# A decoder step on one core: the turn of the normed input, and the state products of two heads together

## The chip, the cores and the metric

The kernel runs on one core of one Trainium2 chip. A core has TensorE (PE; its weight loads are shown apart as PEld), VectorE (DVE), ScalarE (ACT), GpSimd (POOL) and SyncE (SP), which here issues most of the loads. The metric is the device time of one execution in microseconds, as the median of several runs. The traces are of one profiled execution.

## The reference, cut to what matters

One step of a decoder layer for 256 prompt tokens and for 64 sample tokens (8 sequences of 8), with shared weights. The input is normed and goes through one wide projection; its columns feed a gated linear attention (DeltaNet, 32 value heads, one 128 x 128 state per head and sequence) and a sparse attention over cached pages; both meet in an output projection.

```python
h = rmsnorm(x, norm_g)
u = einsum('btd,de->bte', h, w_in)          # 2048 -> 23664 columns
...
def step(s, xs):                            # linear attention, per head
    u_c, w_c, attn_c, qg_c, kdec_c, gl_c = xs
    v_new = u_c - einsum('bhcd,bhde->bhce', w_c, s)
    o = einsum('bhcd,bhde->bhce', qg_c, s) + einsum('bhij,bhje->bhie', attn_c, v_new)
    s = s * gl_c[..., None, None] + einsum('bhcd,bhce->bhde', kdec_c, v_new)
    return s, o
...
y = x + (sigmoid(m_a) * (o_a @ w_branch_a) + sigmoid(m_b) * (o_b @ w_branch_b)) @ w_out
```

For the samples the 8 tokens of a sequence are one chunk, so that each head needs one such step per sequence, from a state that is loaded and stored again.

## The kernel before, in words

All 320 tokens are kept turned: 16 blocks of 128 input columns on the partitions, tokens in the free dimension (`hhi`, `hlo`). Each fp32 product of a weight matrix is made of three products of split numbers: the input and the weights are each cut into a high part of the shorter format (`fp32r`) and the rest (`hi` and `lo`). A tile of 128 output columns (`acc`) thus takes 16 blocks x 3 = 48 products on TensorE; 11,952 such products (with those of the three output matrices) are the bulk of its work. SyncE loads the weights in pieces of 1 MB into three buffers (`p_load`), ScalarE makes the high part (`p_hi`, tiles `whi`), VectorE the low one (`p_lo`, `wlo`; the first four on GpSimd), and `p_mm` issues the products.

Everything else runs beside this as streams: generators that yield the engine and the tiles that their next piece needs. `Run.go` picks the next piece at each point: the one that can start first by the times that the class `Clock` keeps from prices of instructions and loads, and among equals the one of lowest rank. The order so found is the order of each engine's instructions. A piece whose data come later on the chip than `Clock` has it makes its engine wait, and all that is queued behind it. `Next` and `Place` stand for the time when a buffer comes free. `clock.cold` doubles the prices of TensorE.

Three places matter here.

The start: three tiles of tokens (128, 128 and 64 rows) are loaded; ScalarE squares and sums (`x_norm`), VectorE makes the reciprocal root (`ss`). `gain` spreads the norm's weights over all partitions with four products of one row (`gps`) into four tiles `gb`. `x_turn` scales a piece of 512 columns by root and weights (even pieces on VectorE, odd ones on ScalarE and GpSimd), TensorE transposes its four blocks into a bank (`tp`), ScalarE takes the high part out (`hhi`), VectorE the low one (`hlo`). A projection product of block k waits until the piece with block k of all three tiles is there.

The set-up of the linear attention (`g_init`): small tables are loaded (`c4`, the packs `gdn` and `gini`), the convolution's weights are transposed into `bank`, and a product with `selp` from the pack `gini` puts the samples' gates into another order.

The linear attention goes through 16 groups of two heads. `conv`, `norms`, `prep` and `inverse` prepare a group, `g2_stream` runs the prompt's four pieces in sequence (`p` for the state's growth, `ps<-st,wq` and `ps<-vnz,at` for the output), and `g3_stream` does the samples: for each head eight products of the loaded states with `wS`, one per sequence, each into 32 rows of one bank (`ps<-sS,wqx`), the difference from `uS` on VectorE (`vS`), the product with `ats` onto the same bank, the eviction (`oS`), and then the states' update through `four`, `vx` and `pu`. `load_state` loads the next state into one of two buffers when a head is done.

Of the kernel before, what the change touches and what calls it, by code (L numbers as in the profile page):

```python
# [10 lines left out]
F32 = mybir.dt.float32  # L11
# [435 lines left out]
def step(ctx: ExitStack, tc: tile.TileContext, I, O):  # L447
# [172 lines left out]
    g1row = x0.tile([1, DM], F32, name="grow", bufs=1)  # L620
    SY.dma_start(g1row, dram(I["norm_g"], [[DM, 1], [1, DM]]))
# [11 lines left out]
    gb = [x0.tile([P, 512], F32, name=f"gb{q}", bufs=1) for q in range(4)]  # L633

    def gain():

        one = x0.tile([1, P], F32, name="one", bufs=1)
        V.memset(one, 1.0)
        for q in range(4):
            yield ("pe", g1row, Next(x0p, "tp"))  # L640
            ps = x0p.tile([P, 4, P], F32, tag="tp", name="gps").rearrange("p a b -> p (a b)")
            T.matmul(ps, one, g1row[:, 512 * q:512 * q + 512], start=True, stop=True)
            yield "dve"
            V.tensor_copy(gb[q], ps)
# [3 lines left out]
    def x_norm(ti):  # L648
        t0, n = TT[ti]
        xt = xts[ti]  # L650
        ss = x0.tile([P, 3], F32, tag="ss", name="ss")
        yield ("act", xt)
# [8 lines left out]
        newton(ss[:n, 1:2], ss[:n, 0:1], ss[:n, 2:3])  # L661
        ev = clock.last
        for q in range(4):
            run.add(x_turn(ti, xt, ss, q), q - 4, ev)
# [3 lines left out]
    def x_turn(ti, xt, ss, q):  # L668

        t0, n = TT[ti]  # L670
        c = slice(512 * q, 512 * q + 512)
        if q % 2:
            yield "act"
            S.activation(xt[:n, c], xt[:n, c], AF.Copy, scale=ss[:n, 1:2])
            yield "pool"
            G_.tensor_tensor(xt[:n, c], xt[:n, c], gb[q][:n], op=OP.mult)
        else:
            yield "dve"
            V.scalar_tensor_tensor(xt[:n, c], xt[:n, c], ss[:n, 1:2], gb[q][:n], op0=OP.mult, op1=OP.mult)
        ev = clock.last  # L680
# [3 lines left out]
        yield ("pe", ev, Next(x0p, "tp"))  # L684
        tp = x0p.tile([P, 4, P], F32, tag="tp", name="tp")
        for k in range(4):
            kk = q * 4 + k
            T.transpose(tp[:, k, :n], xt[:n, kk * P:kk * P + P], ident[:n, :n])
        yield "act"
        hs = hhi[:, 4 * q:4 * q + 4, t0:t0 + n]  # L690
        S.activation(hs, tp[:, :, :n], AF.Copy)
        yield "dve"
        V.tensor_tensor(hlo[:, 4 * q:4 * q + 4, t0:t0 + n], tp[:, :, :n], hs.bitcast(F32), op=OP.subtract)
        turned[i] = True
        hq[q] += 1
        done["h"] += 1
# [1662 lines left out]
```

## Time and profile before

| | |
|---|---|
| median of 3 runs | 2552.23 us (2551.02 to 2553.23) |
| the profiled execution | 2554.88 us, its span 2553.1 us |
| TensorE busy | 2503.2 us (98%), 22,220 instructions |
| VectorE, ScalarE, GpSimd busy | 1642.9, 1400.0, 415.2 us |
| mean granted clock of TensorE | 0.993 |
| 16 DMA engines | 549 MB, 215 GB/s |

An fp32 product is recorded as two passes (two matrix instructions), a transpose or a product of the split format as one. The recorded time of a product overlaps the next one's, so the distance between two starts tells what one costs. The idle time in brackets at the end of a row is that of the engine just before it, with what ended it. All code that passes through the helper of `Clock` has one line (L331), so instructions are told apart by their tiles.

### The profile page before, as it was taken

How to read it: one execution, taken by the hardware profiler on the slowest of the kernel's cores; microseconds unless marked ns; L12 is line 12 of the kernel's file. 1: busy time of each engine (PE TensorE's matmuls, PEld its weight loads, DVE VectorE, ACT ScalarE, POOL GpSimd, SP SyncE). 2: the span in 40 equal slices, each digit the busy share in tenths (PEclk: the TensorE clock that was granted, in tenths of full speed). 3: DMA queues.
4: the chain of work that ended last, by engine and by line, in shares of the span. 5: the costliest groups of instructions: out<-in, count | busy, mean ns of one | idle time of the engine just before them, and what ended most of it. 6: DMA issues, size and time to landing. Idle time of an engine off the chain costs nothing.

```text
span 2553.1 us, 59455 instructions
## 1 busy us (share of the span) xinstructions
PE 2503.2 (98%) x22220; PEld 2326.4 (91%) x22220; DVE 1642.9 (64%) x4090; ACT 1400.0 (55%) x3290; POOL 415.2 (16%) x991
## 2 busy tenths in 40 slices
PE   7999999999999999999999999999999989999999
PEld 5998789888889999999999999998999979999999
DVE  5554446655665555545887888788897875555544
ACT  5553444444444434435788767777787755544443
POOL 2000001000000000001234334243333232000000
PEclk9999999999999999999999999999999989999999
DMA  6757776888876999966455645565456556766564
GB/s 198 240 164 252 239 253 221 292 304 297 299 257 231 328 314 317 329 208 200 137 170 171 197 134 181 162 188 163 144 161 200 176 166 199 238 185 185 182 195 127
DMA packets 553796, 549.12 MB, mean 215 GB/s; under 512 B 32995, under 2 KB 457108, under 8 KB 553124
## 3 DMA queue, kind: packets, MB, share of 16 engines
q1 hardware_dynamic: 538660, 496.30, 60.8%
q0 software_dynamic: 14848, 49.04, 5.3%
q8 instruction: 175, 2.87, 0.4%
q14 instruction: 113, 0.92, 0.1%
HBM read 472.93 MB, written 72.29 MB: 214 GB/s over the span
## 4 chain that ended last, share of the span: by engine, by line
PE 73%; issue 17%; DVE 4%; POOL 3%; DMA 1%; ACT 1%; SPq 1%; POOLq 0%; DVEq 0%; ACTq 0%
PE acc L331 55%; PE ps L331 6%; PE nt L331 3%; PE op L331 1%; PE pp L331 1%; POOL vx L331 1%; PE ns L331 1%; PE bank L331 1%; PE p L331 1%; PE pu L331 1%; POOL d_mz L299 1%; DVE wlo L331 1%; PE tp L331 1%; PE ms L331 1%; SPq L299 1%
## 5 line engine op out<-in xcount | busy, mean ns | idle before, releaser
L331 PE MATMUL acc<-hhi,whi 128*128 128x320 f32 (+1 forms) x3472 | 1149.3, 331 | 0.5 <-ACT hhi L331 0.5
L331 PE MATMUL acc<-hhi,wlo 128*128 128x320 f32 (+1 forms) x3472 | 1077.7, 310 | 0.0
L331 PE MATMUL acc<-hlo,whi 128*128 128x320 f32 (+1 forms) x3472 | 1076.9, 310 | 0.1
L331 ACT ACTIVATE whi<-wraw 128x512 fp32r<-128x512 f32 (+1 forms) x996 | 625.4, 629 | 795.7 <-PE acc L331 751.2
L331 DVE TENSOR_TENSOR wlo<-wraw,whi 128x512 fp32r<-128x512 f32 x992 | 681.8, 691 | 516.4 <-ACT whi L331 495.2
L331 PEld LDWEIGHTS acc<-hhi,whi 128*128 128x128 f32 (+1 forms) x3472 | 658.3, 190 | 25.0 <-issue 17.4
L331 PEld LDWEIGHTS acc<-hlo,whi 128*128 128x128 f32 (+1 forms) x3472 | 658.5, 190 | 6.7 <-issue 2.4
L331 PEld LDWEIGHTS acc<-hhi,wlo 128*128 128x128 f32 (+1 forms) x3472 | 655.7, 189 | 0.0
L331 PE MATMUL acc<-oal,whi 128*128 128x320 f32 x512 | 158.3, 309 | 0.0
L331 PE MATMUL acc<-oah,wlo 128*128 128x320 f32 x512 | 158.3, 309 | 0.0
L331 PE MATMUL acc<-oah,whi 128*128 128x320 f32 x512 | 158.3, 309 | 0.0
L331 POOL CAST vx<-v 32x128 fp32r<-32x128 f32 x256 | 98.2, 384 | 115.3 <-DVE v L331 85.4
L331 DVE SCALAR_TENSOR_TENSOR cv<-xp,cw,cv 128x344 f32<-128x344 f32 x192 | 110.9, 578 | 6.1 <-ACT cv L331 4.5
L299 POOL DMA_DIRECT2D d_mz<-raw x48 | 26.1, 544 | 493.0 <-ACT raw L331 410.9
L331 PEld LDWEIGHTS acc<-oal,whi 128*128 128x128 f32 x512 | 96.1, 188 | 0.0
L331 PEld LDWEIGHTS acc<-oah,whi 128*128 128x128 f32 x512 | 96.1, 188 | 0.0
L331 PEld LDWEIGHTS acc<-oah,wlo 128*128 128x128 f32 x512 | 96.1, 188 | 0.0
L331 ACT ACTIVATE kT<-nt 128x512 f32<-128x512 f32 x80 | 46.8, 594 | 84.3 <-PE nt L331 84.1
L331 DVE SCALAR_TENSOR_TENSOR sS<-sS,ends,pu 128x128 f32<-128x128 f32 x256 | 83.0, 339 | 14.3 <-PE pu L331 13.9
L331 DVE COPY kT<-nt 128x512 f32<-128x512 f32 x80 | 54.4, 689 | 53.0 <-PE nt L331 52.1
L331 PE MATMUL nt<-pk_const,spg 128*128 128x128 f32 x512 | 74.1, 277 | 2.1 <-DMA d_mz<-raw 2.1
L331 PE MATMUL pp<-cpg,Pk 128*32 128x512 f32 x608 | 75.1, 597 | 0.0
(424 smaller groups left out, 3414.4 us busy)
## 6 DMA issues: line engine op xcount, KB each, us to landing
wraw<-w_in SPq DMA_DIRECT2D x120, 1024.0 KB
wraw<-w_in SPq DMA_DIRECT2D x129, 512.0 KB
cpg<-cache_k_cmp SPq DMA_DIRECT2D x128, 256.0 KB
cpg<-cache_v_cmp SPq DMA_DIRECT2D x128, 256.0 KB
spg<-cache_k_sel SPq DMA_DIRECT2D x128, 256.0 KB
spg<-cache_v_sel SPq DMA_DIRECT2D x128, 256.0 KB
wraw<-w_branch_a SPq DMA_DIRECT2D x32, 1024.0 KB
sS<-state_gdn SPq DMA_DIRECT2D x32, 512.0 KB
```

Of the source, the lines that this page charges most:

```text
L299: return f(*a, **k)
L331: return f(*a, **k)
```

## The change

The norm's weights are loaded as 16 rows of 128 and transposed once into a tile of 16 columns (`gcol`). The root is put on the diagonal of a matrix (`dg`) and the turn of a block is a full fp32 product of the block with it, so that the turn scales too. On the turned side VectorE multiplies four blocks by their four columns of `gcol` (`y`), ScalarE takes the high part from there, and the low part is made on VectorE for even pieces and on GpSimd for odd ones. The rows that the 64-row tile leaves free are set to zero and its root to one. A stream `keep_busy` of rank 20, which is behind all others, issues products of zeros with zeros (`nought`) as long as fewer than eleven pieces are turned, 120 at most; the planner counts TensorE's prices as doubled for the first twenty.

In `g_init` the yields now name the tables that the transposes and the product with `selp` need.

In `g3_stream` both heads' eight products go into two halves of one bank, one after the other; then come one difference of 256 columns, two products with `ats` and one eviction. The states' update is as before, but `four` uses the space of its output and of `vS` instead of tiles of its own. The first product now needs the states of both heads.

```diff
     xts = []
-    g1row = x0.tile([1, DM], F32, name="grow", bufs=1)
-    SY.dma_start(g1row, dram(I["norm_g"], [[DM, 1], [1, DM]]))
+    grow = x0.tile([KT, P], F32, name="grow", bufs=1)
+    SY.dma_start(grow, dram(I["norm_g"], [[P, KT], [1, P]]))
...
-    gb = [x0.tile([P, 512], F32, name=f"gb{q}", bufs=1) for q in range(4)]
+    gcol = x0.tile([P, KT], F32, name="gcol", bufs=1)
+    x0w = pool(x_ctx, "x0w", 1, PSUM)
 
     def gain():
-
-        one = x0.tile([1, P], F32, name="one", bufs=1)
-        V.memset(one, 1.0)
-        for q in range(4):
-            yield ("pe", g1row, Next(x0p, "tp"))
-            ps = x0p.tile([P, 4, P], F32, tag="tp", name="gps").rearrange("p a b -> p (a b)")
-            T.matmul(ps, one, g1row[:, 512 * q:512 * q + 512], start=True, stop=True)
-            yield "dve"
-            V.tensor_copy(gb[q], ps)
+        yield ("pe", grow, ident, Next(x0p, "tp"))
+        ps = x0p.tile([P, 4, P], F32, tag="tp", name="gps")
+        T.transpose(ps[:, 0, :KT], grow, ident[:KT, :KT])
+        yield "dve"
+        V.tensor_copy(gcol, ps[:, 0, :KT])
+
+    def keep_busy():
+
+        zero = x0.tile([P, P], F32, name="zero", bufs=1)
+        ps = x0w.tile([P, P], F32, name="nought")
+        V.memset(zero, 0.0)
+        for i in range(120):
+            yield ("pe", zero)
+            if done["h"] > 10:
+                return
+            T.matmul(ps, zero, zero, start=True, stop=True)
+            clock.cold = i < 20
...
         newton(ss[:n, 1:2], ss[:n, 0:1], ss[:n, 2:3])
+        dg = x0.tile([P, P], F32, name="dg")
+        yield "dve"
+        V.tensor_scalar(dg, ident, ss[:, 1:2], None, op0=OP.mult)
         ev = clock.last
         for q in range(4):
-            run.add(x_turn(ti, xt, ss, q), q - 4, ev)
+            run.add(x_turn(ti, xt, dg, q), q - 4, ev)
...
-    def x_turn(ti, xt, ss, q):
+    def x_turn(ti, xt, dg, q):
 
         t0, n = TT[ti]
-        c = slice(512 * q, 512 * q + 512)
-        if q % 2:
-            yield "act"
-            S.activation(xt[:n, c], xt[:n, c], AF.Copy, scale=ss[:n, 1:2])
-            yield "pool"
-            G_.tensor_tensor(xt[:n, c], xt[:n, c], gb[q][:n], op=OP.mult)
-        else:
-            yield "dve"
-            V.scalar_tensor_tensor(xt[:n, c], xt[:n, c], ss[:n, 1:2], gb[q][:n], op0=OP.mult, op1=OP.mult)
-        ev = clock.last
         yield lambda: len(turned) < 3 or turned[-3]
         i = len(turned)
         turned.append(False)
-        yield ("pe", ev, Next(x0p, "tp"))
+        yield ("pe", dg, Next(x0p, "tp"))
         tp = x0p.tile([P, 4, P], F32, tag="tp", name="tp")
         for k in range(4):
             kk = q * 4 + k
-            T.transpose(tp[:, k, :n], xt[:n, kk * P:kk * P + P], ident[:n, :n])
+            T.matmul(tp[:, k, :n], xt[:, kk * P:kk * P + P], dg[:, :n], start=True, stop=True)
+        yield ("dve", tp, gcol)
+        y = x0.tile([P, 4, P], F32, tag="y", name="y")[:, :, :n]
+        V.tensor_tensor(y, tp[:, :, :n], bc(gcol[:, 4 * q:], [[1, 4], [0, n]]), op=OP.mult)
+        hs = hhi[:, 4 * q:4 * q + 4, t0:t0 + n]
         yield "act"
-        hs = hhi[:, 4 * q:4 * q + 4, t0:t0 + n]
-        S.activation(hs, tp[:, :, :n], AF.Copy)
-        yield "dve"
-        V.tensor_tensor(hlo[:, 4 * q:4 * q + 4, t0:t0 + n], tp[:, :, :n], hs.bitcast(F32), op=OP.subtract)
+        S.activation(hs, y, AF.Copy)
+        e, eng = ("pool", G_) if q % 2 else ("dve", V)
+        yield e
+        eng.tensor_tensor(hlo[:, 4 * q:4 * q + 4, t0:t0 + n], y, hs.bitcast(F32), op=OP.subtract)
...
-    run.add(gain(), -1)
+    run.add(gain(), -6)
+    run.add(keep_busy(), 20)
...
-        yield ("pe", clock.last, Place(clock, bank[:, :384]))
+        yield ("pe", clock.last, c4, Place(clock, bank[:, :384]))
         ps = bank[:, :384]
         for j in range(4):
             T.transpose(ps[:, j * 64:j * 64 + 64], c4[:, j], ident[:64, :64])
+        yield ("pe", E["selp"], D["quad"])
         T.matmul(ps[:, 256:320], E["selp"][:64], bag[:64, 2, :64], start=True, stop=True)
...
-        xT = g1.tile([P, nu, 4, 4, 8], F32, tag=t1, name="xT")
+        own = t1 is None
+        if own:
+            xT = out[:, 0:1].rearrange("p u (a b t) -> p u a b t", a=4, b=4)
+        else:
+            xT = g1.tile([P, nu, 4, 4, 8], F32, tag=t1, name="xT")
...
             o = g1.tile([P, 2, P], F32, tag="oS", name="oS")
+            sts = [sload.pop(2 * j), sload.pop(2 * j + 1)]
+            yield ("pe", wS, *sts, Next(p3, "k"))
+            ps = p3.tile([P, 512], F32, tag="k", name="ps")
             for h in range(2):
-                st = sload.pop(2 * j + h)
-                yield ("pe", wS, st, Next(p3, "k"))
-                ps = p3.tile([P, 512], F32, tag="k", name="ps")
                 for b in range(B):
                     q = 32 * (b % 4)
-                    T.matmul(ps[q:q + 32, :P], wS[:, h, b], st[:, b], start=b < 4, stop=b >= 4)
-                yield "dve"
-                vn = g1.tile([P, P], F32, tag="vS", name="vS")
-                V.tensor_tensor(vn, uS[:, h], ps[:, :P], op=OP.subtract)
-                yield "pe"
-                T.matmul(ps[:, :P], ats[:, h], vn, start=False, stop=True, skip_group_check=True)
-                yield ("act", ps)
-                S.activation(o[:, h], ps[:, :P], AF.Copy)
+                    T.matmul(ps[q:q + 32, h * P:h * P + P], wS[:, h, b], sts[h][:, b], start=h == 0 and b < 4, stop=b >= 4, skip_group_check=True)
+            yield "dve"
+            vn = g1.tile([P, 2, P], F32R, tag="vS", name="vS")
+            V.tensor_tensor(vn.bitcast(F32), uS, ps[:, :256].rearrange("p (h e) -> p h e", h=2), op=OP.subtract)
+            yield "pe"
+            for h in range(2):
+                T.matmul(ps[:, h * P:h * P + P], ats[:, h], vn[:, h].bitcast(F32), start=False, stop=True, skip_group_check=True)
+            yield ("act", ps)
+            S.activation(o.rearrange("p h e -> p (h e)"), ps[:, :256], AF.Copy)
+            for h in range(2):
+                st = sts[h]
                 v4 = g1.tile([P, 2, P], F32, tag="v4", name="v4")
-                yield from four(vn.rearrange("p (u e) -> p u e", u=1), v4, 16, "xTv", "vS")
+                yield from four(vn[:, h:h + 1].bitcast(F32), v4, 16, None, vn[:, h])
```

The order of TensorE's instructions at the start, before: `gps` are the spread weights, `tp` the turned blocks, `acc` projection products (112 columns in the first tile).

```order
L331 MATMUL gps<-grow,one 128x512 x4
L331 MATMUL tp<-pk_const,xt 128x128 x16
L331 MATMUL tp<-pk_const,xt 128x64 x4
L331 MATMUL tp<-pk_const,xt 128x128 x12
L331 MATMUL tp<-pk_const,xt 128x64 x8
L331 MATMUL tp<-pk_const,xt 128x128 x4
L331 MATMUL acc<-hhi,whi 112x320
L331 MATMUL acc<-hlo,whi 112x320
L331 MATMUL acc<-hhi,wlo 112x320
```

After, from behind the turns of the first tile on (`nought` are products of zeros, `dg` the diagonal):

```order
L331 MATMUL nought<-zero 128x128 x8
L331 MATMUL tp<-dg,xt 128x128 x4
L331 MATMUL nought<-zero 128x128 x8
L331 MATMUL tp<-dg,xt 128x128 x8
L331 MATMUL nought<-zero 128x128 x3
L331 MATMUL tp<-dg,xt 128x128 x4
L331 MATMUL nought<-zero 128x128 x12
L331 MATMUL tp<-dg,xt 128x64 x8
L331 MATMUL nought<-zero 128x128 x6
L331 MATMUL tp<-dg,xt 128x64 x4
L331 MATMUL nought<-zero 128x128 x9
L331 MATMUL tp<-dg,xt 128x64 x4
```

Four products of zeros and then the first projection product follow. Ahead of this piece stand 14 products of zeros, the transpose of the weights, 8 more products of zeros and the first tile's 16 turns.

In the set-up of the linear attention, TensorE, as a difference between the two (`+` is after): `bank<-bag,pk_gini` is the product with `selp`.

```order
+L331 MATMUL acc<-hhi,whi 128x320
+L331 MATMUL acc<-hlo,whi 128x320
+L331 MATMUL acc<-hhi,wlo 128x320
+L331 MATMUL acc<-hhi,whi 128x320
+L331 MATMUL acc<-hlo,whi 128x320
+L331 MATMUL acc<-hhi,wlo 128x320
 L331 MATMUL bank<-bag,pk_gini 128x64
 L331 MATMUL acc<-hhi,whi 128x320
```

Before, this product stood right behind the four transposes of the convolution's weights; now twelve projection products stand between, of which the last six are shown.

In the linear attention, TensorE, at the third run of state products (the second group) (`ps<-sS,wqx` for one head; `p` and `vnz` belong to the prompt's pieces):

```order
L331 MATMUL p_18677<-vnz_16007,kde 128x128 x2
L331 MATMUL kq<-kqP 128x128 x2
L331 MATMUL ps<-sS,wqx_15999 32x128 x8
L331 MATMUL ps<-vnz_16007,at 128x128 x2
L331 MATMUL acc<-hhi,whi 128x320
L331 MATMUL acc<-hlo,whi 128x320
L331 MATMUL acc<-hhi,wlo 128x320
L331 MATMUL ps<-vS,ats_16001 128x128
L331 MATMUL acc<-hhi,whi 128x320
L331 MATMUL acc<-hlo,whi 128x320
L331 MATMUL acc<-hhi,wlo 128x320
L331 MATMUL ps<-st,wq 128x128 x2
```

After, at the second group:

```order
L331 MATMUL p_18719<-vnz_16086,kde 128x128 x2
L331 MATMUL ps<-sS,wqx_16078 32x128 x16
L331 MATMUL ps<-vnz_16086,at 128x128 x2
L331 MATMUL kk<-kqP 128x128 x2
L331 MATMUL kk<-kqS 128x128
L331 MATMUL ps<-vS,ats_16080 128x128 x2
L331 MATMUL ps<-st,wq 128x128 x2
L331 MATMUL acc<-hhi,whi 128x320
```

Both heads' sixteen state products stand in one run, and the two products with `ats` in another. From 5250 projection products on, the two orders share next to no place; between 500 and 4770 they are the same.

## Rows read from the trace of the kernel before

**Rows 1.** The page, part 1: busy us (share of span), instructions.

```profile
PE 2503.2 (98%) x22220; PEld 2326.4 (91%) x22220; DVE 1642.9 (64%) x4090; ACT 1400.0 (55%) x3290; POOL 415.2 (16%) x991
```

**Rows 2.** Waits of TensorE, whole span: us in total, times, longest.

```profile
PE tp L331 <- DVE hlo L331: 6.3, 4, 3.5
...
PE bank L331 <- DVE kqP L331: 3.9, 1, 3.9
PE bank L331 <- DMA pk_gini<-c_gini: 3.1, 1, 3.1
```

**Rows 3.** Timeline, 0 to 80 us: start, us, engine, operation [idle before].

```profile
2.70 7.16 PE L331 MATMUL gps<-grow,one 1*128 1x512 f32 x8 [2.70 <-DMA grow<-norm_g]
...
6.14 1.91 ACT L331 ACTIVATE jk<-xt 128x2048 bf16<-128x2048 f32 x1 [4.11 <-DMA xt<-x_prompt]
...
10.66 1.41 DVE L331 SCALAR_TENSOR_TENSOR xt<-xt,ss,gb 128x512 f32<-128x512 f32 x2
11.27 1.91 ACT L331 ACTIVATE jk<-xt 128x2048 bf16<-128x2048 f32 x1 [2.09 <-DMA xt<-x_prompt]
...
17.07 9.21 POOL L331 TENSOR_TENSOR xt<-xt,gb 128x512 f32<-128x512 f32 x6 [16.61 <-DVE ss L331]
...
25.67 4.41 DVE L331 SCALAR_TENSOR_TENSOR xt<-xt,ss,gb 64x512 f32<-64x512 f32 x1
...
41.25 0.31 PE L331 MATMUL acc<-hhi,whi 128*112 128x320 f32 x1
...
43.90 0.31 PE L331 MATMUL acc<-hhi,whi 128*112 128x320 f32 x1
```

**Rows 4.** Timeline of SyncE, 30 to 140 us: its issues of loads.

```profile
54.06 11.89 SPq L299 DMA_DIRECT2D lastB<-d_v  x8
66.05 9.23 SPq L299 DMA_DIRECT2D wraw<-w_in  x3
...
81.37 4.49 SPq L299 DMA_DIRECT2D cpg<-cache_k_cmp  x8
```

**Rows 5.** Timeline of TensorE, 86 to 100 us.

```profile
90.54 2.78 PE L331 MATMUL pp<-cpg,Pk 128*32 128x512 f32 x22
```

**Rows 6.** Timeline of TensorE, 1146 to 1170 us.

```profile
1154.11 0.43 PE L331 MATMUL bank<-pk_const,c 64*128 64x64 f32 x4 [0.43 <-DMA al<-gdn_dt_bias]
1157.62 0.68 PE L331 MATMUL bank<-bag,pk_gini 64*128 64x64 f32 x2 [3.08 <-DMA pk_gini<-c_gini]
1158.23 0.63 PE L331 MATMUL acc<-hhi,whi 128*128 128x320 f32 x1
...
1164.00 0.38 PE L331 MATMUL acc<-hhi,whi 128*128 128x320 f32 x1
```

**Rows 7.** Timeline of TensorE, 2043 to 2082 us.

```profile
2048.53 0.64 PE L331 MATMUL ps<-sS,wqx 128*32 128x128 f32 x16 [0.94 <-issue]
2049.10 0.41 PE L331 MATMUL acc<-hhi,whi 128*128 128x320 f32 x1
...
2066.96 2.05 PE L331 MATMUL ps<-TTf,kb 128*128 128x128 f32 x8 [0.69 <-ACT TTf L331]
2068.66 0.61 PE L331 MATMUL acc<-hhi,whi 128*128 128x320 f32 x1
...
2072.28 1.05 PE L331 MATMUL ps<-vb,TTf 128*128 128x128 f32 x8
2073.09 0.39 PE L331 MATMUL acc<-hhi,whi 128*128 128x320 f32 x1
```

**Rows 8.** Timeline of TensorE, 2116 to 2124 us.

```profile
2118.42 0.71 PE L331 MATMUL p<-vnz,kde 128*128 128x128 f32 x4
...
2122.28 0.64 PE L331 MATMUL p<-vnz,kde 128*128 128x128 f32 x4
```

**Rows 9.** Windows: length, busy us of PE, PEld, DVE, ACT, POOL, PEclk, DMA.

```profile
1757.00:1773.00 16.00, 11.31 (x57) 10.13 (x56) 14.48 (x51) 6.08 (x19) 7.12 (x20) 0.79 0.52 175
2050.00:2073.00 23.00, 17.04 (x217) 14.25 (x216) 15.17 (x54) 13.39 (x47) 6.71 (x19) 0.63 0.63 200
```

More of the change, by code (lines that the diff above doesn't have):

```diff
@@ L651, in x_norm @@
         ss = x0.tile([P, 3], F32, tag="ss", name="ss")
+        if n < P:
+            V.memset(ss, 1.0)
+            G_.memset(xt[n:], 0.0)
         yield ("act", xt)
@@ L1783, in four @@
             V.transpose(xT[:, u].rearrange("p a b t -> p b a t"), x[:, u])
-        hl = g1.tile([P, nu, 2, 4, 2, 8], F32R, tag=t2, name="hl")
+        if own:
+            hl = t2.rearrange("p (u a b k t) -> p u a b k t", u=1, a=2, b=4, k=2)
+        else:
+            hl = g1.tile([P, nu, 2, 4, 2, 8], F32R, tag=t2, name="hl")
         xv = bc(xT, [[128, nu], [8, 8], [1, 8]])
```

## The prediction

> **What bounds the kernel now.** I read the page's busy shares first, then the waits of TensorE, then its timeline where those waits lie. The page has TensorE busy for 98% of the span [rows 1]. Its longest waits are few and lie in three places: the first forty microseconds, where the turned input comes late (6.3 us in four waits), the set-up of the linear attention (3.1 us for one table) and the linear attention itself (one wait of 3.9 us) [rows 2]. Everywhere else projection products follow one another: 18 intervals between 41.25 and 43.90 us are 0.147 us each [rows 3]. So time is gained by starting the run of products earlier, by taking work or breaks out of TensorE's row, or by taking away one of its waits; what VectorE or ScalarE save counts only through these. The change touches all three places. The order of TensorE's rows tells more: between product 500 and product 4770 of the 11,952 projection products it is the same in both kernels, so that nothing but a shift is to be expected there.
>
> **The start.** Before, the 19th projection product starts at 41.25 us [rows 3]. What holds it back is the scaling of the input ahead of the turn: VectorE scales a piece in 0.70 us when alone (1.41 for two), but one piece of half the rows takes 4.41 us while GpSimd multiplies its six pieces (9.21 us, 1.53 each) [rows 3]. The Trainium skill (SBUF — State Buffer, "SBUF: two separate sides") says that a GpSimd operation and a VectorE operation with two inputs in SBUF exclude each other for a whole instruction; the 4.41 against 0.70 agrees.
>
> After, the scale by the root goes into TensorE: twelve turns are full fp32 products with a diagonal matrix, and 72 products of zeros stand between them. TensorE itself is then what bounds the start. Its prices: eight passes of fp32 products, that is four products of 128 columns, take 0.81 us from 2072.28 to 2073.09, or 0.20 each; four at the lower clock take 1.70 us from 2066.96 to 2068.66, or 0.425 each [rows 7]. The second tile's square starts at 11.27 and ends at 13.2. In before the first tile needs 2.6 us from the end of its square (8.05) to the first scaled piece (10.66) [rows 3]; one eviction of 0.7 us of the first tile comes between now, so the second diagonal is there at about 16.6. From there TensorE's row, as the order shows it, holds 42 zero products and 16 turns of 128 columns (58 at 0.20: 11.8 us) and 16 turns of 64 columns. These have no row; half the columns would be 0.10, the same weights to load 0.20, and I take 0.20, as all rows of fp32 have the weights loaded per pass: 3.2 us. The run of products then begins at 16.6 + 15.0 = 31.6. Up to the 19th lie 18 x 0.147 and one fp32 product of 383 columns (three times 0.20), which stands before the 19th in both: 34.9. Against 41.25 that is 6.3 earlier; I take **-6 us**.
>
> Bounds: if the zero products cost nothing the vector chain decides. GpSimd then has six low parts and four weight pieces at 1.53, 15.3 us from about 14.5, and the last quarter of the columns is wanted 36 products (5.3 us) after the first, so the run could begin at 25: -12. If the clock stays at the lower level all 104 fp32 products of 128 columns take 0.425: from 1.3 us on that is 44.2, with the small ones 48 to 50, and the 19th product starts 14 us later than before: +14. Which it is hangs on whether products of zeros raise the clock. In before the eight passes over a single row kept TensorE busy for 7.16 us [rows 3]; that they raised anything no row shows. After the wait at 1157.62 the first 21 products stand 0.275 apart (1158.23 to 1164.00) [rows 6], the lower of the two levels (1.2 GHz), and then the clock rises while only products run. I take it that the zero products, which follow one another as those do, raise it.
>
> The Trainium skill (TensorE: Matmul & The Clock Gate, "Part 1: The HAM clock gate") says that the slow state is the default and that activity releases it. The wait at 1157 agrees. By that rule, if products of zeros are activity, the sum above holds.
>
> **The set-up of the linear attention.** The order moves one product behind twelve projection products. TensorE waited 3.08 us for its table [rows 6]; twelve at 0.147 fill 1.8 of that. The 21 products after the wait then lose 21 x (0.275 - 0.147) = 2.7 us to the lower clock; with a wait of 1.3 us left I count most of it as gained. **-4 us**, between -1.8 (the clock falls all the same) and -5.8; a loss is excluded unless the table comes later than in before, since the loads keep their place on SyncE.
>
> **The state products.** Eight products of a head take 0.57 us (2048.53 to 2049.10) and the projection product behind them 0.41 instead of 0.31 [rows 7], so a break costs about 0.1 on leaving, and I take as much on entering. Sixteen in one run keep the work, and save one such break per group: 16 x 0.2 = 3.2 us; the second product pair saves a similar break only where it stood alone. One subtraction and one eviction per group fall away, on engines that TensorE does not wait for here. **-3 us**, between 0 (the breaks come back elsewhere; +5 with late states, below) and -6. What the joint run adds is a wait: both heads' states must be there before the first product, and the second of them is loaded only when the group before has stored its own. Behind that product all of TensorE's row is queued. The planner knows of this wait and places the run by its own load times; I cost it at nothing. Should the load be late for one group in four, at 2 us each, it is 8 us, and the term turns to +5.
>
> **The waits in the linear attention.** From 5250 products on the order differs throughout. Two places of before lost time: from 1757 to 1773 TensorE was busy for 11.3 of 16 us with the granted clock at 0.79, and from 2050 to 2073 for 17.0 of 23 at 0.63 [rows 9]. The idle 4.7 and 6.0 us and about half of the time at half clock (0.21 x 2 x 16 = 6.7 and 0.37 x 2 x 23 = 17.0 us) make some 19 us. The second place stood in the order as two runs of five groups that wait for each other without a projection product between; after, no such run is left there. But after has a run of 32 groups at product 6672, with a whole chain of four pieces of the state recurrence. One step of that chain takes 3.86 us even with other work between (2118.42 to 2122.28) [rows 8]; three steps and the groups ahead make 13 us, with some 9.8 us of work of TensorE in them (31 products at 0.20, sixteen small ones 1.1, the rest 2.5). So 3 to 10 us are lost there, the larger if the clock falls. The first place of before stood in no long run of the order: VectorE was late there (busy 14.5 of 16 us [rows 9]), and that can come back anywhere. From a gain of 19, less 3 to 10 for the run and as much again for places not foreseen, I keep **-5 us**, between -16 and +8.
>
> **Sum.** -6 - 4 - 3 - 5 = -18 us. The profiled execution took 2554.88 us, 2.65 above the median of the three runs; 2554.88 - 18 is 2536.9, and 2.65 less, against the median, 2534.
>
> **Rivals.** (1) New waits in the linear attention: VectorE bounds that stage, and what TensorE saves comes back as waits for full input buffers. For it: 14.5 of 16 us busy [rows 9], and the run of 32 groups. Against it: TensorE lost only 20% there. Then the last term is +8 instead of -5: 2547. (2) The zero products don't raise the clock, and TensorE comes to the first product 14 us later than before; the other terms don't make that good: -18 + 6 + 14 = +2, 2554, slower than before, and slower still with any new wait. It decides if the run of products begins after some 43 us. For it: no row shows what zeros do. Against it: the rise behind 1164. (3) The loads do not keep up with the earlier start. The order asks for the cache's first pages after 201 products instead of 297, that is 14 us earlier and 6 for the start; TensorE came to them at 90.54 [rows 5], 4.7 us after their last issue at 85.9. SyncE has the eight table loads (11.89 us) ahead of them and one weight load less (9.23 us for three, so 3), and the vector that these tables are read from is ready after 51 products instead of 72, 3 us earlier and 6 for the start [rows 4]: 12 against 20, of which 4.7 less the time to land are spare, so 3 to 5 us of waits, 2538. A like loss comes if the six low parts left on VectorE each wait for a GpSimd operation of up to 1.53 us, as 4.41 against 0.70 suggests [rows 3]: 9 us on a vector chain that would end at about 26 (16.6 and some fourteen operations of up to 0.70), so 3 us of the start's gain. The rule of the Trainium skill quoted above (SBUF — State Buffer) would make just that of it. (4) Both lossy places vanish and the start is nearer its lower bound: 2520.
>
> **Chances.** Forecast 0.48; (1) 0.20; (2) 0.08; (3) 0.12; (4) 0.12. What a measurement of this kernel can tell from no change is 0.2%, 5.1 us, so faster means under 2547.1. The forecast but for a small part, (3), (4) and half of (1) are faster: 0.80; same 0.12, from (1) and half of (2); slower 0.08, from (2) with new waits and the far end of (1). The range for 8 in 10 is 2517 to 2551: it reaches over (4) and (1) and leaves out (2) and the far ends of the waits. The forecast's own range is 2525 to 2543.
>
> **What would show it.** The 19th product at 33 to 37 us, with 0.147 between the products from the first on (right) or 0.27 (rival 2). One wait of under 1.5 us for the table at about 1150, and no granted clock of half behind it. Sixteen runs of 32 passes of the state products, about 1.1 us each. A busy share below 0.8 in a stretch of 15 us at product 6672, and none at the end of the linear attention. The prediction is wrong if the time is above 2551, or if the gain comes from the middle of the program, where the order is the same.

## The result, and the profile after

After: 2536.77 us, the median of four runs (2536.47 to 2540.34), against 2552.73 for before beside it: a ratio of 0.9943, 95% interval 0.993 to 0.9956 (the quotient of the two medians is 0.9937). The profiled execution has a span of 2534.7 us, 18.4 less than before's; between the medians lie 16.0. Where these come from is read best by the time at which the n-th projection product starts: 4.5 us earlier at the 19th, 2.8 at the 500th and unchanged to about the 2000th, 3.3 at the 4770th, 7.9 at the 4800th, 18.35 at the 9300th and to the end.

The page, part 1 and 4 of after, for [rows 1]: TensorE has 185 instructions more (144 of them passes of zeros) and 1.3 us more busy time in a span that is 18 us shorter.

```profile
PE 2504.5 (99%) x22405; PEld 2337.8 (92%) x22405; DVE 1636.3 (65%) x4075; ACT 1398.0 (55%) x3268; POOL 414.1 (16%) x992
...
PE 89%; DVE 4%; issue 3%; DMA 2%; ACT 1%; POOL 1%; SPq 0%; DVEq 0%; ACTq 0%; POOLq 0%
```

The start, timeline of TensorE, for [rows 3]: `nought` are the zeros (two passes each), `tp<-dg` the turns. The last row is the 19th projection product.

```profile
1.09 5.89 PE L331 MATMUL nought<-zero 128*128 128x128 f32 x28 [1.09 <-DVE ss L331]
...
7.08 2.05 PE L331 MATMUL nought<-zero 128*128 128x128 f32 x16
...
13.74 1.95 PE L331 MATMUL nought<-zero 128*128 128x128 f32 x16
16.57 1.13 PE L331 MATMUL tp<-dg,xt 128*128 128x128 f32 x8 [0.89 <-issue]
17.54 1.95 PE L331 MATMUL nought<-zero 128*128 128x128 f32 x16
19.32 1.95 PE L331 MATMUL tp<-dg,xt 128*128 128x128 f32 x16
...
25.36 1.90 PE L331 MATMUL tp<-dg,xt 128*128 128x64 f32 x16
27.09 1.56 PE L331 MATMUL nought<-zero 128*128 128x128 f32 x12
...
33.09 0.39 PE L331 MATMUL acc<-hhi,whi 128*112 128x320 f32 x1
...
36.74 0.31 PE L331 MATMUL acc<-hhi,whi 128*112 128x320 f32 x1
```

The first 28 passes take 5.89 us, 0.21 each; the 16 from 7.08 on, with one small transpose between, take 2.05, or 0.13 each, and from 17.54 to 19.32 they stand 0.111 apart. The trace lists the stretches of granted clock; the first, at full, begins at 6.38 us, when TensorE had run nothing but zeros: products of zeros did raise the clock. From 16.57 to 33.09 TensorE has no idle time worth a bracket. It is the bound, as forecast.

What the start gains lies for the most part behind the first product. That one stands at 33.09 us, and before at 33.84, only 0.75 later; from it to the 19th it is 3.65 us now, and 7.41 before. In before the first such stretch at full clock begins at 41.15 us, and up to there the products stand 0.27 apart, as those behind the wait at 1157 do (0.275, [rows 6]). Rows and windows of before's TensorE (a window's granted clock reads 1.00 where the trace has no record of it): busy all the time, it does 17 passes from 35 to 40 us and 33 from 45 to 50.

```profile
33.84 0.61 PE L331 MATMUL acc<-hhi,whi 128*112 128x320 f32 x1
...
34.25 0.47 PE L331 MATMUL acc<-hlo,whi 128*112 128x320 f32 x1
...
34.52 0.47 PE L331 MATMUL acc<-hhi,wlo 128*112 128x320 f32 x1
```
```profile
35.00:40.00 5.00, 5.00 (x17) 3.27 (x18) 2.42 (x4) 1.92 (x3) 1.80 (x3) 1.00 0.79 241
...
45.00:50.00 5.00, 5.00 (x33) 4.29 (x32) 2.26 (x8) 3.90 (x8) 0.00 (x0) 1.00 0.01 2
```

The cache's first pages, for [rows 5], and the set-up of the linear attention, for [rows 6]:

```profile
71.08 4.29 PE L331 MATMUL pp<-cpg,Pk 128*32 128x512 f32 x22
...
1150.43 0.43 PE L331 MATMUL bank<-pk_const,c 64*128 64x64 f32 x4
1150.80 0.41 PE L331 MATMUL acc<-hhi,whi 128*128 128x320 f32 x1
...
1154.36 0.43 PE L331 MATMUL bank<-bag,pk_gini 64*128 64x64 f32 x2 [1.54 <-DMA pk_gini<-c_gini]
1154.72 0.42 PE L331 MATMUL acc<-hhi,whi 128*128 128x320 f32 x1
```

The pages take 1.5 us longer than before (4.29 against 2.78), and the weight loads of these products wait five times, 2.3 us in all, for the pages' DMAs. The wait for the table is 1.54 us instead of 3.08.

The linear attention, for [rows 7] and [rows 9]. Groups by line and shape of TensorE in after, then in before (count | busy us, mean ns | idle before):

```profile
L331 PE MATMUL ps<-sS,wqx 128*32 128x128 f32 x512 | 18.1, 282 | 1.0 <-DMA sS<-state_gdn 1.0
L331 PE MATMUL ps<-vS,ats 128*128 128x128 f32 x64 | 10.4, 287 | 0.6 <-DVE vS L331 0.6
```
```profile
L331 PE MATMUL ps<-sS,wqx 128*32 128x128 f32 x512 | 20.6, 279 | 1.1 <-issue 1.1
L331 PE MATMUL ps<-vS,ats 128*128 128x128 f32 x64 | 13.0, 284 | 0.8 <-DVE vS L331 0.8
```

The sixteen runs have 32 passes each, of 1.08 us where nothing comes between; the state products' own busy time falls by 2.5 us. (The recorded times of neighbours overlap, so what the second row falls by is not all saved.) Then windows of after: the two places where before lost time, the run of 32 groups (1520.0 to 1536.3), and a new place.

```profile
1757.00:1773.00 16.00, 16.00 (x143) 15.54 (x142) 14.90 (x47) 11.81 (x34) 2.11 (x10) 1.00 0.26 87
2050.00:2073.00 23.00, 21.77 (x156) 19.85 (x157) 18.80 (x66) 14.56 (x45) 5.68 (x15) 0.85 0.49 160
1520.00:1536.30 16.30, 13.12 (x114) 10.86 (x113) 15.67 (x54) 9.59 (x28) 5.81 (x15) 1.00 0.20 60
2047.00:2058.00 11.00, 8.16 (x61) 6.60 (x61) 7.10 (x26) 6.18 (x19) 1.46 (x3) 0.69 0.64 210
```

The first place is gone, the second has shrunk to the 11 us around 2050, and the long run idles for 3.2 of its 16.3 us at full clock.

### The profile page after: what moved, and what is told of

The parts are those of the page before. It is cut to its first block, busy times and chain, and to the rows that moved or that the text cites. A ratio compares the mean times of both kernels' runs of the same rounds, so it can differ in the third digit from the quotient of the medians.

```text
span 2534.7 us, 59791 instructions
## 1 busy us (share of the span) xinstructions
PE 2504.5 (99%) x22405; PEld 2337.8 (92%) x22405; DVE 1636.3 (65%) x4075; ACT 1398.0 (55%) x3268; POOL 414.1 (16%) x992
## 4 chain that ended last, share of the span: by engine, by line
PE 89%; DVE 4%; issue 3%; DMA 2%; ACT 1%; POOL 1%; SPq 0%; DVEq 0%; ACTq 0%; POOLq 0%
PE acc L331 64%; PE ps L331 6%; PE nt L331 4%; PE op L331 3%; PE pp L331 3%; PE ns L331 2%; PE tp L331 2%; PE sp L331 1%; PE bank L331 1%; PE p L331 1%; PE pu L331 1%; PE ms L331 1%; POOL vx L331 1%; DVE wlo L331 1%; PE nought L331 0%
## 5 line engine op out<-in xcount | busy, mean ns | idle before, releaser
L331 DVE SCALAR_TENSOR_TENSOR sS<-sS,ends,pu 128x128 f32<-128x128 f32 x256 | 84.2, 338 | 11.3 <-PE pu L331 10.4
```

What stands on the lines that cost most here:

```text
L331: return f(*a, **k)
```

## The experiments

Orders of instructions are compared by what stands between the n-th and the next projection product. By that the three parts of the change are independent: the order at the start hangs on the start's part alone, that of the set-up on the set-up's, that of the linear attention, but for six places with products of the set-up, on the state products' alone.

**The start alone** (`e1_start`): before, with the hunks on `gain`, `keep_busy`, `x_norm` and `x_turn`.

```diff
+    run.add(gain(), -6)
+    run.add(keep_busy(), 20)
```

> Before with the change of the start alone (diagonal turns, products of zeros, columns of the norm's weights). The order of TensorE's row is that of after up to product 4770 and that of before from there on. Theory (the three parts are independent and their gains add): the 19th projection product at 36.7 us as in after, 4.5 us earlier than before, of which the late pages of the cache give 1.5 us back; 2.8 us earlier from product 500 to the end, ratio 0.9989. Rival (what is gained at the start shifts the later work against its loads, and so makes the gain of the linear attention): the linear attention changes too, 9 to 13 us faster in all, ratio 0.995 to 0.9965.

2549.05 us, ratio 0.998 (0.9971 to 0.9989), so that the gain is clear of the noise; 0.9989 was expected. The 19th product at 36.61 us, 3.4 us gained at the 500th. A pair of traces does not size this gain, though: with before's start product 500 stands at 124.8 to 128.3 us in five traces (before, `e2`, `e3`, `e8`, `e11`), with after's at 124.4 to 128.4 in four (after, `e1`, `e6`, `e7`). In the earliest of before's (`e8`) the clock is full from 35.25 us on and the 19th product stands at 37.89, by the same instructions. The linear attention takes 986.3 us from the 4800th to the 9300th product, against 988.4 in before and 977.9 in after: the rival is out.

**The set-up alone** (`e2_init`):

```diff
+        yield ("pe", E["selp"], D["quad"])
         T.matmul(ps[:, 256:320], E["selp"][:64], bag[:64, 2, :64], start=True, stop=True)
```

> Before with the change of the set-up alone (the wait for the table named, so that twelve projection products go ahead of the product with selp). Theory: the wait falls from 3.1 to about 1.5 us and the granted clock does not fall behind it; 4.65 us gained between product 4770 and 4771 to 4790, nothing elsewhere, ratio 0.9982. Rival (the clock's fall is only moved): 1.8 us, ratio 0.9993.

2548.95 us, ratio 0.998 (0.9971 to 0.9989). The wait for the table is 1.26 us, the clock stays full behind it, and 4.5 us are gained between product 4770 and 4800 (0.9 more this execution had from its start). As the theory had it.

**The state products alone** (`e3_states`):

```diff
+            sts = [sload.pop(2 * j), sload.pop(2 * j + 1)]
+            yield ("pe", wS, *sts, Next(p3, "k"))
```

> Before with the change of the state products alone; the order of TensorE's row in the linear attention is that of after, everywhere else that of before. Theory (parts add; the gain of the linear attention hangs on its order alone, not on when it starts): 10.4 us gained between product 4771 and 9300, half-clock time behind product 4771 falls from 24 to 10 us, ratio 0.9959. Rival (the order helps only since the linear attention starts 7 us earlier against its loads): 0 to 5 us gained, ratio 0.998 to 1.000.

2540.88 us, ratio 0.9947 (0.9934 to 0.9961). The linear attention takes 977.4 us, 10.9 less than in before. So its gain does not need the earlier start. (From product 4800 to 9300 the clock is at half for 3.4 us, against 24 in before and 10 in after.) By places the three parts give 3.4, 4.5 and 10.9 us, 18.8 together, and after has 18.4; by the ratios they multiply to more (0.9907, against after's 0.9943 and, below, 0.9929). The three intervals reach together to 0.9939, which takes in the second of these and only with after's own interval the first. So that the parts add up is borne out by the places, and not to better than 6 to 9 us by the times; I have no cause for the surplus.

**No zeros** (`e4_nozero`): after, without the stream.

```diff
-    run.add(keep_busy(), 20)
```

> After without the products of zeros, else the same order from product 500 on. Theory (zeros raise the clock but stand in the way, since TensorE's row bounds the start from 16 us on): without them the turns take 0.4 us each, the run of products begins at about 30 us at the lower clock and loses 3 to 4 us until it rises; the 19th product at 35 to 38 us, the whole within 3 us of after, 2534 to 2540, ratio to before 0.993 to 0.9955. Rival (the zeros are what the start's gain rests on): the 19th product at 41 us or later as in before, the whole 4.5 us above after, 2541 or more, ratio 0.9955 or more.

2533.92 us, ratio 0.9915 (0.9901 to 0.9929). The run of products begins at 29.39 us and the 19th stands at 34.79, 2 us earlier than in after. The zeros weren't needed for the start's gain: the turns, which begin at 10.11 us, raise the clock themselves, to full from 15.74 us on. TensorE then stands idle for 4.16 us ahead of the third tile, and works at half clock behind that, up to 29.39 us. Its row at that place, and windows of this kernel:

```profile
22.56 7.01 PE L331 MATMUL tp<-dg,xt 128*128 128x64 f32 x32 [4.16 <-DVE dg L331]
```
```profile
16.00:23.00 7.00, 2.84 (x24) 2.68 (x23) 6.22 (x12) 3.28 (x8) 5.86 (x5) 0.97 1.13 354
23.00:30.00 7.00, 7.00 (x36) 7.00 (x36) 4.23 (x8) 2.88 (x5) 2.65 (x3) 0.54 0.39 80
```

So the theory holds that zeros stand in the way; at the start they cost 2 us more than they give. All three traces without zeros (`e4`, `e9`, `e10`) have product 500 at 121.4 to 122.3 us, ahead of all four with them. The forecast of the whole time was missed: the ratio lies below 0.993 to 0.9955.

**Zeros at the front only** (`e5_zeros_early`):

```diff
-        for i in range(120):
+        for i in range(22):
```

> After with 22 products of zeros in place of 72: all of them stand ahead of the first turn, none behind it. Theory (72 zeros cost the start some 50 passes pairs of 0.12 to 0.2 us in TensorE's row, and the run without any lost 6.8 us at half clock instead): the clock is full from about 6 us and stays so, the turns take 0.2 us each, the run of products begins at 26 to 30 us and the 19th stands at 29 to 33 us, 2 to 5 us faster than the run without zeros over the first 500 products. Rival (the clock falls in the gaps between the turns, so that early zeros give nothing): the 19th at 34 to 36 us as without zeros.

2531.14 us, ratio 0.991 (0.9892 to 0.9927), but the start is not what the theory made of it: the 19th product stands at 35.47, between the two, and the rival is right on that. The theory fell: the clock was not full throughout. It fell to half at 17.8 us and, after a rise, again at 24.7; the mean of the granted clock was 0.67 from 20 to 30 us and 0.59 from 30 to 36. TensorE had waited 2.44 us and 1.68 us between the turns ahead of these falls:

```profile
16.40 5.44 PE L331 MATMUL tp<-dg,xt 128*128 128x128 f32 x32 [2.44 <-issue]
23.52 6.08 PE L331 MATMUL tp<-dg,xt 128*128 128x64 f32 x32 [1.68 <-DVE y L331]
```

The ratio can't be told from that without zeros (0.9915).

**After again** (`e6_after_again`), unchanged.

> After, unchanged, beside the other kernels of this call. Theory (its zeros cost more than they give): 2 to 4 us slower than after without zeros had been against its own before, ratio to before 0.9935 to 0.9945; the gap of 16.3 us between product 6672 and 6673 comes again, since it lies in the order. Rival (the gap was one execution's): it is below 10 us.

2535.68 us, ratio 0.9929 (0.9911 to 0.9946). The gap between product 6672 and 6673 is 16.3 us again. This profiled execution shows how much the start varies: its 19th product stands at 40.91 us. ScalarE's square of the second tile began when its load landed, at 12.95 us; in the first profile of after that was at 10.40. The zeros that the order puts ahead of that tile were done, TensorE waited 3.42 us, and the clock was half from 19.4 to 22.8 us.

```profile
12.95 1.91 ACT L331 ACTIVATE jk<-xt 128x2048 bf16<-128x2048 f32 x1 [4.23 <-DMA xt<-x_prompt]
```

**The joint wait taken apart** (`e7_split_wait`): the eight products of each head wait for their own state.

```diff
-            yield ("pe", wS, *sts, Next(p3, "k"))
+            yield ("pe", wS, sts[0], Next(p3, "k"))
...
             for h in range(2):
+                yield ("pe", sts[h])
```

> After, but the sixteen state products wait for their states in two steps, the first head's eight for the first state and the other eight for the second; the rest of the planning is open, and the order of the linear attention is another one, without a run of 32 groups. Theory (the joint wait costs next to nothing, 1.0 us in one wait; the order as a whole decides): the linear attention (product 4800 to 9300) differs from after by a few us of either sign, with no wait for a state gone that was worth more than 1 us. Rival (the joint wait is what the run of 32 groups comes from, and what holds the linear attention back): 5 to 10 us faster than after.

2541.11 us, ratio 0.9948 (0.9929 to 0.9967). No run of 32 groups is left, and the linear attention takes 985.7 us, 7.7 more than in after. So parting the joint wait did not pay, and the rival is out. What the long run alone costs is not shown by it, since the whole order changed along with it. The state products' busy time is 20.2 us here, since the planner parts 14 of the 16 runs.

**Other orders of the same instructions.** Two of before (`e8_before_reordered` with TensorE, `e11_before_second_order` with VectorE), two of after without zeros (`e9_second_order`, and `e10_recurrence_first`, where `g2_stream` goes first among equals). The first three only move a number by which the planner thinks an engine busy:

```diff
+                clock.t["pe"] += 75      # e8; e11: clock.t["dve"] += 75
+            clock.t["pe"] += 150         # e9
-    run.add(g2_stream())                 # e10
+    run.add(g2_stream(), -1)
```

> Before, with one number of the planner moved: it takes TensorE as 75 ns busier ahead of each head's state products. Instructions and data are the same, the order of the linear attention differs nearly throughout. Theory (the gain of the state products' change in the linear attention is for the most part another draw of the order): the time moves by several us, 3 to 12 of either sign, between product 4800 and 9300. Rival (the joint products themselves give the gain): within 2 us of before.

> After without the products of zeros, and with one number of the planner moved: it takes TensorE as 150 ns busier ahead of each joint run of state products. Instructions are those of the run without zeros; the order of the linear attention shares next to no place with it. Theory (the orders of the same instructions lie several us apart in the linear attention, and after's is a lucky or a middling one of them): between product 4800 and 9300 it takes 3 to 10 us more or less than without this. Rival (the joint products and not the order decide): within 1.5 us of it, that is 10 to 12 us less than before.

> After without the products of zeros, and with the stream of the prompt's recurrence (p, ps<-st,wq, ps<-vnz,at) preferred among pieces that can start at the same time (rank -1). Another order of the same instructions. Theory as for the second order: 3 to 10 us of either sign between product 4800 and 9300 against the run without zeros; faster by as much if the recurrence, as the longest chain, is what the linear attention waits for. Rival (order is of no matter): within 1.5 us.

> Before, with one number of the planner moved: it takes VectorE as 75 ns busier ahead of each head's state products. A second other order of before's own instructions. Theory (orders decide): between product 4800 and 9300 again some us off before, of either sign; with the first one 4 us less. Rival (before's orders are all alike, and only the joint products bring 10 us): within 1.5 us of before.

Ratios to before: `e8` 0.9974 (0.9964 to 0.9983), `e9` 0.9951 (0.9935 to 0.9968), `e10` 0.9992 (0.9983 to 1.0002), `e11` 0.9971 (0.9961 to 0.9981). Windows from product 4800 to product 9300, in this order: before, after, `e11`, `e9`, `e10`. Columns as in [rows 9]: the length, then TensorE's busy time.

```profile
1165.24:2153.60 988.36, 968.05 (x9334) 918.16 (x9332) 792.07 (x2316) 719.83 (x1959) 330.82 (x844) 0.99 0.55 169
```
```profile
1157.31:2135.25 977.94, 962.27 (x9333) 916.48 (x9332) 792.42 (x2304) 721.67 (x1946) 330.34 (x844) 0.99 0.56 172
```
```profile
1165.04:2144.61 979.57, 964.78 (x9333) 913.91 (x9332) 791.66 (x2317) 719.46 (x1960) 330.48 (x844) 1.00 0.55 171
```
```profile
1151.73:2138.65 986.92, 965.15 (x9333) 917.67 (x9332) 789.88 (x2304) 719.28 (x1946) 331.58 (x844) 0.99 0.55 171
```
```profile
1152.39:2150.41 998.02, 967.37 (x9334) 921.06 (x9332) 798.14 (x2312) 726.98 (x1954) 322.70 (x844) 0.99 0.55 171
```

TensorE does the same passes in all five. Before's instructions take 979.6 to 988.4 us there (984.4 in `e8`), after's 975.5 to 998.0. One and the same order repeats to 4 us: 986.3, 987.4 and 988.4 in three traces of before's, 975.5 to 979.4 in six of after's. The joint runs are as short in the bad orders as in after (17.4 us of busy time in `e9`, 17.3 in `e10`). What differs most between orders of the same instructions is TensorE's idle time: 20.3 us in before and 14.8 in `e11`; 15.7 in after, 21.8 in `e9` and 30.7 in `e10`. Of the 10.4 us from before to after 4.6 are idle time and 5.8 busy time, 2.5 of these in the state products. Recurrence first makes it wait 10.0 us for `vx` from GpSimd, where after waits 3.1:

```profile
PE pu L331 <- POOL vx L331: 10.0, 17, 2.2
PE ps L331 <- DVE TTd L331: 5.5, 4, 3.7
PE ps L331 <- DVE R L331: 3.3, 1, 3.3
```

The order, then, moves this stage by as much as the whole change of the state products, and by more: `e9` and `e10` took 11 and 22 us more than the run without zeros (976.0), more than the 3 to 10 expected (`e10` was to be faster if the stage waited for the recurrence), and `e8` and `e11` 4 and 9 us less than before. After's order was the best of its four (with `e7`), and before's the worst of its three. The mean of before's three orders is 984 us, that of after's four 987. So these runs don't show that joint products make the stage faster as such; with so few orders they don't rule out a few us either.

**Zeros where TensorE stands idle** (`e12_zeros_in_gap`): after without its stream; 18 zeros behind the sixth turn.

```diff
+        if i == 5:
+            for _ in range(18):
+                T.matmul(nought, zero, zero, start=True, stop=True)
```

> After without its stream of zeros; 18 products of zeros are placed by hand behind the sixth turn, where the run without zeros left TensorE idle for 4.16 us ahead of the third tile's first turn and went on at half clock. Theory (zeros are worth something only where TensorE would stand idle, and cost their time elsewhere): the clock does not fall at 22 us, the third tile's turns take 0.2 us each, the run of products begins 2 to 4 us earlier than without zeros, at 25.5 to 27.5 us, the 19th at 30.5 to 33 us, the linear attention as in after (976 to 979 us between product 4800 and 9300); 2528 to 2532 us, ratio to before 0.990 to 0.992. Rival (VectorE and GpSimd are what the first product waits for): the run begins at 29 us as without zeros, and TensorE waits ahead of it.

2528.41 us, ratio 0.9911 (0.9894 to 0.9927): the lowest median of all, though its ratio is that of the runs without zeros and with zeros at the front (0.9915, 0.991). The run of products begins at 26.14 us and the 19th stands at 32.77, the earliest of all, with the clock full from 15.57 us on. TensorE's timeline:

```profile
10.09 8.22 PE L331 MATMUL tp<-dg,xt 128*128 128x128 f32 x48 [3.05 <-DVE dg L331]
18.15 4.18 PE L331 MATMUL nought<-zero 128*128 128x128 f32 x36
22.57 3.75 PE L331 MATMUL tp<-dg,xt 128*128 128x64 f32 x32 [0.24 <-DVE dg L331]
...
26.14 0.38 PE L331 MATMUL acc<-hhi,whi 128*112 128x320 f32 x1
```

The same 32 passes of turns took 7.01 us in the run without zeros. From 18.15 to 22.33 us, which the zeros fill, the run without them waited for the third diagonal. The theory holds for the start, which is worth 1 to 2 us more than without zeros (120.3 us at product 500, against 121.4 to 122.3 in three traces). That the whole program is faster by it is not shown: the rest of the 5.5 us between the two medians is not the start's, and the ratios are the same.

## Why the prediction was right, and where not

The forecast was 2534 us, and 2536.77 was measured; its sum was -18, against 18.4 us gained in the profiled execution and 16.0 between the medians. That the sum came so near is in part luck: the start gave about 3 us less than its term, the linear attention 2.4 more than its two. The steps:

**The start, -6: the bound right, the size off, and the gain not where it was said to be.** 4.5 us at the 19th product, which came at 36.74 instead of 34.9. The step that was mis-sized is the price of a product: 74 products from 16.57 to 33.09 are 0.223 each, not 0.20, which makes 16.5 us of the 15.0. And the prediction looked at before's 19th product alone, and took the scaling ahead of the turn to be what holds it back. Before's first product already stood at 33.84 us, and the 7.41 us from there to the 19th were spent at the lower clock. So 0.75 of the 4.5 us come from an earlier begin, and 3.8 from what lies between the first and the 19th product, above all from the clock (18 products at 0.27 instead of 0.147 us make 2.2 of it). That a turn of 64 columns costs what one of 128 does was right: 16 passes of 64 columns take 1.73 us (25.36 to 27.09), 0.108 each, against 0.111. Then 1.5 us more went at the pages: that is the third rival's mechanism, forecast at 3 to 5 us and given 0.12. I treated it as a case of its own; it happened beside the forecast, and a part of it belonged into the sum. The lock on VectorE came too, without effect on the end: while GpSimd made the weights' low parts, a low part of the input took 1.63 us and the third diagonal 1.16, where 0.68 and 0.28 were enough before that. For the low part this agrees with the rule quoted in the prediction (the Trainium skill, SBUF — State Buffer, "SBUF: two separate sides").

```profile
16.20 0.28 DVE L331 TENSOR_SCALAR dg<-pk_const,ss 128x128 f32<-128x128 f32 x1
...
19.73 0.68 DVE L331 TENSOR_TENSOR hlo<-y,hhi 128x512 fp32r<-128x512 f32 x1
20.33 1.16 DVE L331 TENSOR_SCALAR dg<-pk_const,ss 128x128 f32<-128x128 f32 x1
21.41 1.63 DVE L331 TENSOR_TENSOR hlo<-y,hhi 128x512 fp32r<-128x512 f32 x1
```

The second rival (the clock stays low) fell. But so did a thing that the prediction took along with it: that the start needs the zeros. Without them it was faster.

**The set-up, -4:** 4.65 us between product 4770 and 4800. The wait was 1.54 us (forecast 1.3), and behind it the clock did not fall. Right.

**The state products, -3:** 2.5 us of busy time of the runs, and the joint wait cost 1.0 us once. Right as far as the busy time of these rows tells; the time from start to start, which counts the gaps as well, gives 1.2 (19.2 against 18.0). That the stage as a whole gains by them is not shown, as the other orders tell.

**The waits in the linear attention, -5: the sum right, the reason not shown.** The linear attention gained 10.4 us, so some 8 besides the state products. The lossy places of before went or shrank as forecast, the run of 32 groups idled 3.2 us (forecast 3 to 10). That no such stretch would be left at the end was wrong: from 2038 to 2053 TensorE was busy for 10.8 of 15 us, and from 2047 to 2058 for 8.2 of 11 at a clock of 0.69, held up by `vnz` and by the second head's state:

```profile
2049.99 0.71 PE L331 MATMUL p<-vnz,kde 128*128 128x128 f32 x4 [1.71 <-POOL vnz L331]
2050.63 0.82 PE L331 MATMUL ps<-sS,wqx 128*32 128x128 f32 x16
2052.46 1.08 PE L331 MATMUL ps<-sS,wqx 128*32 128x128 f32 x16 [1.01 <-DMA sS<-state_gdn]
```

The 19 us that the term set out from are not the sum of its parts either: 10.7 us idle and half of 23.7 us at half clock make some 22.5. And the runs of other orders show that the term can't be read from the change: three other orders of after's instructions took 8 to 20 us more than after's, and two of before's 4 to 9 us less than before's. Another order than after's can lie beyond the bound of +8: in `e10` the linear attention took 9.7 us more than in before with the state products' 2.5 us saved, so that the term is +12 there. The first rival (1) is of that kind, and I gave it 0.20. So the term came near in part by luck: with another order of the same instructions it would have been missed.

## What to carry to other kernels

Where a planner sets the order, run a second order of the same instructions before crediting a local edit with what a whole stage gained. Fill TensorE with idle work only in gaps that the trace of the kernel without it shows, for the same filler in a row that has become the bound delays what stands behind it: the 19th product came at 36.74 us with 72 zeros, at 34.79 with none and at 32.77 with 18 in the gap. Look at the clock of the kernel before as well: a start can look late since it runs at half clock. Sum up small rivals that can happen together with the forecast, instead of giving each a chance against it.

## What was not expected of the hardware

Products of zeros raise the clock: it was full from 6.38 us on, with passes of zeros and nothing else before, and a pass then took 0.13 us, and soon 0.111, instead of 0.21. This agrees with the Trainium skill (TensorE: Matmul & The Clock Gate, "Part 1: The HAM clock gate"), that the slow state is the default and activity releases it. In the run without zeros the clock fell from full to half at 22.56 us, behind 4.16 us in which TensorE stood idle, and the turns there took 7.01 us where 3.75 do at full clock.

The landing of a load at the start differs between executions of the same program by 2.5 us (10.40 and 12.95 us for the second tile), and this, with the half clock that followed the wait, moved the 19th product by 4.2 us, more than the whole gain of that part at product 500.
